# Both attentions of a Trainium2 network: score products issued in pairs, float32 operands kept whole, and the parallel layer's sums of squares by matmul

## The chip, the cores and the metric

The kernel runs on one core of one Trainium2 chip. Its time is the device time of one execution in microseconds (us), and the figure to compare is the median over runs. The engines are named as the profile names them: PE is TensorE, PEld its weight loads, DVE is VectorE, ACT is ScalarE, POOL is GpSimd, SP issues DMAs.

## The reference, cut to what matters

A network of four layers over one sequence of 512 positions with 1,024 features, all in float32, each layer followed by a SwiGLU feed-forward block. Layer 0 is an mLSTM, layer 3 a short convolution; the change does not touch them. Two layers hold an attention.

Layer 1, the window attention (16 query heads of 64, 4 key heads, blocks of 128 queries that see the block before, their own and the next):

```python
scores = jnp.einsum('bcqhgd,bckhd->bchgqk', q, k_band) * (hd ** -0.5)
scores = jnp.where(mask[None, :, None, None], scores, -jnp.inf)
m = jnp.maximum(jnp.max(scores, axis=-1), sink_l)
p = jnp.exp(scores - m[..., None])
denom = jnp.sum(p, axis=-1) + jnp.exp(sink_l - m)
out = jnp.einsum('bchgqk,bckhd->bcqhgd', p, v_band)
```

Layer 2, the parallel layer, runs an attention and a state-space model (SSM) from one input projection. The attention (8 heads of 64, causal) first picks, with 8 small index heads, the 128 best keys of each query, and then attends to those alone:

```python
il = jnp.einsum('bthd,bsd->bths', iq_blk, ik) * (IDX_DIM ** -0.5)
score = jnp.einsum('bths,bth->bts', jax.nn.relu(il), iw_blk)
_, sel = lax.top_k(score, topk)
q_lat = jnp.einsum('bthd,hdc->bthc', q_blk, w_uk)
logits = jnp.einsum('bthc,btkc->bthk', q_lat, c_sel) * (HEAD_DIM_A ** -0.5)
p = jax.nn.softmax(logits, axis=-1)
```

Ahead of layer 2 stand two norms one behind the other: the first block's final norm (weight `fin`) and layer 2's own (weight `par`).

## The kernel before, in words

Activations lie with features on the partitions: `xT[0..7]` are eight tiles of 128 features by 512 positions. A large product is not done in whole float32. Each operand is split into a high and a low part in the rounded type `fp32r` (`whi`/`wlo` for weights, `xh`/`xl` for activations), and three products of these parts stand for one: lines 206 to 208 (`mm3`), 212 to 214 (`mm3n`). Such a product over 512 columns is called a gemm product below, and they are by far the most of PE's work. The splitting costs ACT one pass (line 171) and DVE or POOL another (line 166) for each weight tile.

Products of heads are 64 rows deep. Two heads stand in one tile, one on partitions 0 to 63 and one on 64 to 127 (`halves`).

PSUM's eight banks are dealt to four uses, `g`, `s`, `t` and `o`; `bank(tag)` takes the next bank of a use in turn. `s` holds scores, `t` transposes, `o` attention outputs, `g` gemm products.

**Window attention** (`window`, lines 949 to 1075). `attend(g, c, y)` does four heads for one block `c` of queries: line 1015 multiplies queries by 256 keys (c = 0 and 3) or 384 keys (c = 1 and 2) in whole float32; line 1020 (DVE) adds the mask and takes the row minimum; line 1023 (ACT) is the exponential; line 1027 transposes it block by block; lines 1030 and 1032 copy it out of PSUM (`pT`); line 1036 multiplies by the values, 64 output rows for each of the two halves; lines 1038 to 1050 divide. There are 16 such calls. Six gemm groups (the later queries, `rope`) and six blocks of the output projection (`add_block`) are issued between them and serve PE as other work. In whole float32 one product shows as two PE records.

**Parallel layer** (`parallel`). `norm("par", pre="fin")` makes for each of the eight `xT` tiles two squares on ACT (line 271), two running sums on DVE (line 272), a multiplication by `fin` (line 277) and the split `xh`/`xl` (lines 279, 280). `col_sums` (line 239) adds each running sum over the partitions with four products by a column of ones. From them come two inverse square roots (lines 229 to 234), and `rows` (line 245) spreads these over the partitions as `rb`, which the projection's results are multiplied by. The index weights need a transpose of the first result (line 1124). The index scores (lines 943, 944) use the queries stacked with their low part (lines 929, 930) and the key in two forms (`ikh`, `ikl`). `topk_rounds` picks the best keys on DVE (lines 1176, 1177), a few rounds at a time by `pump`. In the attention itself `att_head(c, h, ...)` does one head for one block: three products of parts for the scores (line 1380), DVE mask and minimum (1381), ACT scale and exponential (1386, 1387), transposes (1391), a split of the result into `pth` (ACT, 1393) and `ptl` (DVE, 1394), and three products of parts by the values for each 128 keys (1402), an odd head with 128 output rows, an even one with 64. `fill` issues gemm groups of the SSM in between.

What is written in one order in the program is not the order on the engines: a scheduler arranges the instructions of all engines by its own estimate of times when the kernel is built. On the chip each engine then goes through its list in that order, and an instruction whose input is not there holds up all behind it.

Of the kernel before, what the change touches and what calls it, by code (L numbers as in the profile page):

```python
# [16 lines left out]
P = 128  # L17
# [40 lines left out]
def tile_net(ctx: ExitStack, tc: tile.TileContext, d, out, layers=(0, 1, 2, 3)):  # L58
# [24 lines left out]

    def bank(tag):
        ids, n = banks[tag]
        banks[tag][1] = (n + 1) % len(ids)
        return pp.tile([P, 512], F32, tag=f"b{ids[n]}", name=f"ps_{tag}", bufs=1)

# [25 lines left out]

    V = nc.vector
# [138 lines left out]

    def norm(wname, pre=None, tag="t", later=False):
# [6 lines left out]
        sums = [scr("ssum", bufs=1)]  # L262
        if pre:
            sums.insert(0, row_tile())
# [9 lines left out]
        for k in range(KT):  # L274
            if pre:
                square(k, sums[0])
                V.tensor_scalar(xT[k], xT[k], col(pre, k), None, op0=ALU.mult)
            hi, lo = xs_pair()
            A.activation(hi, xT[k], AF.Copy, scale=col(wname, k))
            V.scalar_tensor_tensor(lo, xT[k], col(wname, k), hi.bitcast(F32), op0=ALU.mult, op1=ALU.subtract)  # L280
            xs.t.append((hi, lo))
            square(k, sums[-1])
        rcs = []

        def scales():
            for i, ssum in enumerate(sums):
                v = scr("nv", (P, NCH))
                V.tensor_scalar(v, col_sums(ssum, tag), 1.0 / D, None if i else EPS, op0=ALU.mult,
# [658 lines left out]
    def window():  # L947
# [52 lines left out]
        share([1, 3, 3, 1])  # L1000
        halves = slice(0, 64), slice(64, P)

        def attend(g, c, y):
# [8 lines left out]
            for j in range(2):  # L1012
                pss = [bank("s") for _ in halves]
                for a, ps in zip(halves, pss):
                    T.matmul(ps[:, 0:n], lhsT=Q[2 * g + j][a, sl], rhs=K[pair][a, ks], start=True, stop=True)  # L1015
                for r, ps in enumerate(pss):
# [6 lines left out]
                    A.activation(p[:, 0:n], ps[:, 0:n], AF.Exp, scale=-1.0, bias=nmx[:, i:i + 1],  # L1023
                                 accum_out=den[:, i:i + 1])
# [52 lines left out]
    def parallel(after_final):  # L1077
# [3 lines left out]
        QS, CKV, IQ, Z, XBC = 0, 512, 768, 1280, 2304  # L1081

# [37 lines left out]
        V.tensor_tensor(ikw[0:72], p0[0:72], xs.rb[0:72], op=ALU.mult)  # L1120

        cps = bank("t")
        for c in range(NCH):
            T.transpose(cps[:, c * 8:(c + 1) * 8], ikw[64:72, c * P:(c + 1) * P], ident[64:72, 64:72])
        iw = lpool.tile([P, NCH, 8], F32, name="iw")
        V.scalar_tensor_tensor(iw, cps[:, 0:32].rearrange("p (c k) -> p c k", c=NCH), H ** -0.5,
                               xs.rc[:, :, None].to_broadcast([P, NCH, 8]), op0=ALU.mult, op1=ALU.mult)
        ikh, ikl = scr("ikh", dt=F32R, bufs=1), scr("ikl", dt=F32R, bufs=1)
        key_stack(ikw, 0, ikh, ikl)
# [13 lines left out]

        def index(b):
            r = iq[b]
            for par in range(2):
                h = 2 * b + par
                q2 = scr("q2", dt=F32R)
                pair_stack(r, par, q2)
                for c in range(1, NCH):  # L1150
                    n = (c + 1) * P
                    ps = bank("s")
                    scores(ps[:, 0:n], q2, par, ikh, ikl, slice(c * P, (c + 1) * P), slice(0, n))
                    t = scr("rel", bufs=2)
                    A.activation(t[:, 0:n], ps[:, 0:n], AF.Relu, scale=0.125)
# [109 lines left out]
        def keep_q(ps):  # L1265
            hi, lo = keep("N", F32R), keep("N", F32R)
# [476 lines left out]
```

## Time and profile before

| | |
|---|---|
| median of 3 runs | 2445.88 us (2444.16 to 2448.54) |
| profiled execution, its own time | 2444.67 us |
| its span, first to last instruction | 2442.9 us |
| PE busy | 2387.8 us, 98% |
| DVE busy | 1804.2 us, 74% |
| ACT busy | 1198.3 us, 49% |
| POOL busy | 361.2 us, 15% |
| mean granted PE clock | 0.99 of full speed |

The profiled execution is 1.2 us below the median, and 1.8 us of it lie outside the span. A busy PE is not a PE at its peak: a record runs from the start of a product to its modelled end, and records of neighbours overlap. What a product costs PE is therefore read from start to start: the next row's start minus its own.

### The profile page before, as it was taken

How to read it: one execution, taken by the hardware profiler on the slowest of the kernel's cores; microseconds unless marked ns; L12 is line 12 of the kernel's file. 1: busy time of each engine (PE TensorE's matmuls, PEld its weight loads, DVE VectorE, ACT ScalarE, POOL GpSimd, SP SyncE). 2: the span in 40 equal slices, each digit the busy share in tenths (PEclk: the TensorE clock that was granted, in tenths of full speed). 3: DMA queues.
4: the chain of work that ended last, by engine and by line, in shares of the span. 5: the costliest groups of instructions: out<-in, count | busy, mean ns of one | idle time of the engine just before them, and what ended most of it. 6: DMA issues, size and time to landing. Idle time of an engine off the chain costs nothing.

```text
span 2442.9 us, 36706 instructions
## 1 busy us (share of the span) xinstructions
PE 2387.8 (98%) x13956; PEld 2055.9 (84%) x13956; DVE 1804.2 (74%) x3063; ACT 1198.3 (49%) x2226; POOL 361.2 (15%) x252
## 2 busy tenths in 40 slices
PE   8999999999999999999899989999999999999998
PEld 7898899998656899999677867888989788899997
DVE  7676798777564787877789778786867755668877
ACT  4444545454464554545566564553635324445444
POOL 2210001010320001010354145100100010000100
PEclk9999999999999999999999999999999999999999
DMA  5332232323211232323222132232323323223232
GB/s 167 117 100 61 78 117 96 113 87 119 82 51 35 69 113 88 120 87 110 78 71 61 53 111 87 87 100 82 121 87 104 104 96 100 81 88 120 87 104 78
DMA packets 73440, 226.64 MB, mean 93 GB/s; under 512 B 10336, under 2 KB 14576, under 8 KB 73264
## 3 DMA queue, kind: packets, MB, share of 16 engines
q1 hardware_dynamic: 68896, 220.00, 28.0%
q10 hardware_dynamic: 4320, 4.21, 0.6%
q8 instruction: 109, 1.79, 0.3%
q14 instruction: 67, 0.55, 0.1%
q0 software_dynamic: 48, 0.10, 0.0%
HBM read 219.45 MB, written 2.20 MB: 91 GB/s over the span
## 4 chain that ended last, share of the span: by engine, by line
PE 90%; DVE 5%; DMA 2%; ACT 1%; issue 1%; POOL 0%; ACTq 0%; SPq 0%; POOLq 0%; DVEq 0%
PE ps_g L206 7%; PE ps_g L208 7%; PE ps_g L207 7%; PE ps_s L206 4%; PE ps_s L208 4%; PE ps_s L207 4%; PE ps_g L446 4%; PE ps_g L444 4%; PE ps_g L445 4%; PE ps_t L206 3%; PE ps_t L207 3%; PE ps_t L208 3%; PE ps_t L446 3%; PE ps_t L445 3%; PE ps_t L444 3%; PE ps_s L1015 2%
## 5 line engine op out<-in xcount | busy, mean ns | idle before, releaser
L171 ACT ACTIVATE whi<-wraw 128x512 fp32r<-128x512 f32 (+1 forms) x726 | 447.3, 621 | 667.7 <-PE ps_g L207 236.6
L166 DVE TENSOR_TENSOR wlo<-wraw,whi 128x512 fp32r<-128x512 f32 x666 | 490.3, 746 | 188.5 <-ACT whi L171 176.1
L206 PE MATMUL ps_g<-xh,whi 128*128 128x512 f32 (+1 forms) x696 | 279.7, 404 | 2.9 <-DVE ct L1611 2.1
L424 POOL TENSOR_TENSOR S<-wraw 128x1024 f32<-128x1024 f32 x36 | 106.9, 2971 | 1173.3 <-DMA wraw<-in_in_dram 760.3
L207 PE MATMUL ps_g<-xl,whi 128*128 128x512 f32 (+1 forms) x696 | 278.1, 400 | 0.0
L208 PE MATMUL ps_g<-xh,wlo 128*128 128x512 f32 (+1 forms) x696 | 277.8, 399 | 0.0
L171 ACT ACTIVATE whi<-S 128x512 fp32r<-128x512 f32 x288 | 178.2, 628 | 191.3 <-PE ps_g L445 58.2
L166 DVE TENSOR_TENSOR wlo<-S,whi 128x512 fp32r<-128x512 f32 x288 | 199.8, 719 | 34.8 <-ACT whi L171 32.9
L444 PE MATMUL ps_g<-thi,whi 128*128 128x256 f32 x576 | 164.1, 285 | 2.7 <-ACT whi L171 1.9
L446 PE MATMUL ps_g<-thi,wlo 128*128 128x256 f32 x576 | 164.1, 285 | 0.2
L206 PEld LDWEIGHTS ps_g<-xh,whi 128*128 128x128 f32 (+1 forms) x696 | 132.1, 190 | 37.8 <-issue 5.6
L445 PE MATMUL ps_g<-tlo,whi 128*128 128x256 f32 x576 | 163.7, 284 | 0.0
L208 PEld LDWEIGHTS ps_g<-xh,wlo 128*128 128x128 f32 (+1 forms) x696 | 132.0, 190 | 31.6 <-issue 4.4
L207 PEld LDWEIGHTS ps_g<-xl,whi 128*128 128x128 f32 (+1 forms) x696 | 132.2, 190 | 29.1 <-issue 3.5
L444 PEld LDWEIGHTS ps_g<-thi,whi 128*128 128x128 f32 x576 | 111.4, 193 | 3.3 <-ACT whi L171 2.1
L446 PEld LDWEIGHTS ps_g<-thi,wlo 128*128 128x128 f32 x576 | 111.4, 193 | 0.7 <-DVE wlo L166 0.7
L445 PEld LDWEIGHTS ps_g<-tlo,whi 128*128 128x128 f32 x576 | 111.3, 193 | 0.0
L166 POOL TENSOR_TENSOR wlo<-wraw,whi 128x512 fp32r<-128x512 f32 (+1 forms) x60 | 81.0, 1359 | 153.4 <-ACT whi L171 110.5
L207 PE MATMUL ps_s<-hlo,whi 128*128 128x512 f32 x264 | 102.8, 389 | 0.0
L208 PE MATMUL ps_s<-hhi,wlo 128*128 128x512 f32 x264 | 102.7, 389 | 0.0
L206 PE MATMUL ps_t<-hhi,whi 128*128 128x512 f32 x264 | 102.7, 389 | 0.0
L207 PE MATMUL ps_t<-hlo,whi 128*128 128x512 f32 x264 | 102.7, 389 | 0.0
(545 smaller groups left out, 6641.2 us busy)
## 6 DMA issues: line engine op xcount, KB each, us to landing
wraw<-in_in_dram SPq DMA_DIRECT2D x176, 512.0 KB, 3.5
wraw<-in_down_dram SPq DMA_DIRECT2D x82, 512.0 KB, 3.6
wraw<-in_par_in_dram SPq DMA_DIRECT2D x30, 512.0 KB, 3.3
wraw<-in_mlstm_in_dram SPq DMA_DIRECT2D x24, 512.0 KB, 3.6
wraw<-in_sc_in_dram SPq DMA_DIRECT2D x24, 512.0 KB, 3.5
wraw<-in_attn_in_dram SPq DMA_DIRECT2D x12, 512.0 KB, 3.4
wraw<-in_par_out_dram SPq DMA_DIRECT2D x12, 512.0 KB, 3.5
mb<-drs SPq DMA_DIRECT2D x16, 256.0 KB, 4.1
```

The costliest lines, as they stand in the source:

```text
L166: (V if e == "V" else G).tensor_tensor(lo, x, hi.bitcast(F32), op=ALU.subtract)
L171: A.activation(hi, raw, AF.Copy)
L206: T.matmul(o, lhsT=w[0], rhs=x[0], start=start, stop=False)
L207: T.matmul(o, lhsT=w[0], rhs=x[1], start=False, stop=False)
L208: T.matmul(o, lhsT=w[1], rhs=x[0], start=False, stop=stop)
L424: G.tensor_tensor(live[jj, "S1"], live[jj, 2], live[jj, 3], op=ALU.add)
L444: T.matmul(o, lhsT=w[0], rhs=x[i][0], start=start and i == j == 0, stop=False, skip_group_check=True)
L445: T.matmul(o, lhsT=w[0], rhs=x[i][1], start=False, stop=False, skip_group_check=True)
L446: T.matmul(o, lhsT=w[1], rhs=x[i][0], start=False, stop=end, skip_group_check=True)
L1015: T.matmul(ps[:, 0:n], lhsT=Q[2 * g + j][a, sl], rhs=K[pair][a, ks], start=True, stop=True)
```

## The change

It touches both attentions and the entry of the parallel layer.

1. **Pairs.** `side_by_side` issues the score products of two heads (the two halves) one behind the other, at a raised scheduling priority. A dependency is added from each to the instruction that last reads either of their banks (the exponential, or the index heads' ReLU), so that neither starts before both banks are free. `rotate` sets the order in which the `s` banks are taken. In the window attention one bank moves from `t` to `s` (3 and 3 become 4 and 2). In the parallel layer there are three `s` banks, taken as 0 and 1, then 0 and 2.
2. **Whole float32.** In the parallel layer the index scores, attention scores and the products by the values use unsplit operands, each head on its half of the array. The high and low parts of queries, keys, values and probabilities are no longer made. Of two halves the products by the values issue the second first, in both attentions.
3. **Entry.** For `norm("par", pre="fin")` there is one square for each tile instead of two and no running sum. The square itself is the weight side of four small products for each tile, with two columns of weights (ones, and `fin` squared), which add up both sums in PSUM. The split uses one scale, `fin` times `par` (`pcol`, made once at the start on POOL). The multiplication of `xT` by `fin` joins that by the first norm's row and moves into the attention's blocks c = 2 and 3 (DVE, eight instructions, held behind the mask instruction of the pair). The transposes of the index weights move behind the first latent gemm group.

The core of the diff:

```diff
+    def side_by_side(products, tag="s"):
+        tiles, ids = [], []
+        for _ in products:
+            names, n = banks[tag]
+            ids.append(names[n])
+            tiles.append(bank(tag))
+        with tc.high_priority(HP):
+            for f, ps in zip(products, tiles):
+                ins = f(ps)
+                for i in ids:
+                    if i in busy:
+                        tc.add_manual_dep(ins.ins, busy[i].ins.name, SYNC)
+        return list(zip(ids, tiles))
...
-        for k in range(KT):
-            if pre:
-                square(k, sums[0])
-                V.tensor_scalar(xT[k], xT[k], col(pre, k), None, op0=ALU.mult)
...
+        if pre:
+
+            both = bank(tag)
+            for k in range(KT):
+                sq = row_tile()
+                A.activation(sq, xT[k], AF.Square)
+                hi, lo = xs_pair()
+                A.activation(hi, xT[k], AF.Copy, scale=pcol[:, 2 * KT + k:2 * KT + k + 1])
...
+                for c in range(NCH):
+                    T.matmul(both[:, 2 * c:2 * c + 2], lhsT=sq[:, c * P:(c + 1) * P], rhs=pcol[:, 2 * k:2 * k + 2],
+                             start=k == c == 0, stop=k == KT - 1, skip_group_check=True)
...
-        share([1, 3, 3, 1])
+
+        share([1, 4, 2, 1])
+        rotate("s", (0, 1, 2, 3, 1, 0, 3, 2))
...
-                pss = [bank("s") for _ in halves]
-                for a, ps in zip(halves, pss):
-                    T.matmul(ps[:, 0:n], lhsT=Q[2 * g + j][a, sl], rhs=K[pair][a, ks], start=True, stop=True)
-                for r, ps in enumerate(pss):
+                pss = side_by_side([lambda ps, a=a: T.matmul(ps[:, 0:n], lhsT=Q[2 * g + j][a, sl], rhs=K[pair][a, ks],
+                                                             start=True, stop=True) for a in halves])
+                for r, (bid, ps) in enumerate(pss):
...
-                for r, a in enumerate(halves):
+                for r, a in ((1, halves[1]), (0, halves[0])):
...
+        rotate("s", (0, 1, 0, 2))
+
         def index(b):
-            r = iq[b]
-            for par in range(2):
-                h = 2 * b + par
-                q2 = scr("q2", dt=F32R)
-                pair_stack(r, par, q2)
-                for c in range(1, NCH):
-                    n = (c + 1) * P
-                    ps = bank("s")
-                    scores(ps[:, 0:n], q2, par, ikh, ikl, slice(c * P, (c + 1) * P), slice(0, n))
-                    t = scr("rel", bufs=2)
-                    A.activation(t[:, 0:n], ps[:, 0:n], AF.Relu, scale=0.125)
+
+            for c in range(1, NCH):
+                n = (c + 1) * P
+                pss = side_by_side([lambda ps, a=a: T.matmul(ps[:, 0:n], lhsT=iq[b][a, c * P:n], rhs=ik[a, 0:n],
+                                                             start=True, stop=True) for a in halves])
...
-            for i, (x, z) in enumerate(((0, 0), (1, 0), (0, 1))):
-                T.matmul(ps[:, 0:n], lhsT=q[x][a, c * P:n], rhs=k[z][a, 0:n], start=i == 0, stop=i == 2)
...
+            pss = side_by_side([lambda ps, a=a: T.matmul(ps[:, 0:n], lhsT=q[a, c * P:n], rhs=k[a, 0:n],
+                                                         start=True, stop=True) for a in halves])
...
-            A.activation(hi[:, 0:n], pt[:, 0:n], AF.Copy)
-            V.tensor_tensor(lo[:, 0:n], pt[:, 0:n], hi[:, 0:n].bitcast(F32), op=ALU.subtract)
...
+                if par and c >= 2:
+                    V.tensor_copy(t[:, 0:n], pt[:, 0:n])
+                else:
+                    A.activation(t[:, 0:n], pt[:, 0:n], AF.Copy)
...
-                m = P if h % 2 else 64
-                for i, (v, t) in enumerate(((vh, hi), (vh, lo), (vl, hi))):
-                    T.matmul(o[0:m, h // 2 * P:h // 2 * P + P], lhsT=v[:, 0:m], rhs=t[:, sl],
-                             start=j == 0 and i == 0, stop=j == c and i == 2)
+                for par, a in ((1, halves[1]), (0, halves[0])):
+                    T.matmul(o[a, b * P:(b + 1) * P], lhsT=va[j][:, P * b + 64 * par:P * b + 64 * par + 64],
+                             rhs=pts[par][:, sl], start=j == 0, stop=j == c)
...
+                if after_final and c >= 2:
+                    k = 4 * (c - 2) + b
+                    with tc.issue_after(latest[0].ins):
+                        V.scalar_tensor_tensor(xT[k], xT[k], col("fin", k), xs.rb1, op0=ALU.mult, op1=ALU.mult)
```

What the scheduler makes of it, at three places. A row is one instruction as it stands in an engine's list, or so many alike in a row (`x2`); `q_6592` and the like are single tiles of queries and keys.

PE in the gemm-poor middle of the window attention, before (scores line 1015, transposes 1027 and 1047, products by the values 1036):

```order
L1015 MATMUL ps_s<-q_6592,q_6738 128x384
L1027 MATMUL ps_t<-ident,prob 128x128 x6
L1015 MATMUL ps_s<-q_6592,q_6836 128x384 x2
L1047 MATMUL ps_t<-ident,rdb 128x128 x2
L1036 MATMUL ps_o<-pT,va 64x256
L1027 MATMUL ps_t<-ident,prob 128x128 x3
L1015 MATMUL ps_s<-q_6592,q_6738 128x256
L1036 MATMUL ps_o<-pT,va 64x256 x5
```

The same place in the changed kernel, where these lines are 1059 (scores), 1072 and 1092 (transposes) and 1081 (values):

```order
L1059 MATMUL ps_s<-q_6596,q_6840 128x256 x2
L1072 MATMUL ps_t<-ident,prob 128x128 x9
L1059 MATMUL ps_s<-q_6629,q_6958 128x256 x2
L1092 MATMUL ps_t<-ident,rdb 128x128 x2
L1081 MATMUL ps_o<-pT,va 64x256 x6
L1072 MATMUL ps_t<-ident,prob 128x128 x2
```

Over the whole window attention the 64 score products stood alone 41 times, in twos 10 times and once in a three, 52 groups; now twice alone and 31 times in twos, 33 groups. The 80 products by the values stood in groups of 1 (11 times), 3 (6), 4 (2), 5 (5) and 6 (3); now of 1 (once), 3 (once), 4 (7) and 6 (8). The transposes are the same in number.

PE in the parallel attention's last block, before, where two heads of one pair are multiplied by the values (line 1402; 128 output rows for the odd head, 64 for the even one):

```order
L1402 MATMUL ps_o<-ptl,N 128x128
L1402 MATMUL ps_o<-pth,N 128x128 x2
L1402 MATMUL ps_o<-ptl,N 128x128
L1402 MATMUL ps_o<-pth,N 128x128
L1402 MATMUL ps_o<-pth,N 64x128
L1402 MATMUL ps_o<-ptl,N 64x128
L1402 MATMUL ps_o<-pth,N 64x128 x2
L1391 MATMUL ps_t<-ident,prob 128x128 x8
L1380 MATMUL ps_s<-kh,N 128x512 x2
L1380 MATMUL ps_s<-kl,N 128x512
```

In the changed kernel, in the block before the last and at the turn to the last (values 1449, transposes 1439, scores 1424, gemm products 231 to 233):

```order
L1449 MATMUL ps_o<-pth,N 64x128 x6
L1439 MATMUL ps_t<-ident,prob 128x128 x6
...
L1424 MATMUL ps_s<-kh,N 128x512 x2
L231 MATMUL ps_g<-xh,whi 128x512
L232 MATMUL ps_g<-xl,whi 128x512
L233 MATMUL ps_g<-xh,wlo 128x512
L1439 MATMUL ps_t<-ident,prob 128x128 x3
L1449 MATMUL ps_o<-pth,N 64x128 x6
```

Where 240 products by the values stood in runs broken by other work, 80 now stand in groups of 2 (twice), 4 (5 times), 6 (4) and 8 (4), of which each two beside each other are two halves. All 16 score pairs of the attention and all 12 of the index heads stand as twos; the index heads had 24 times two products of parts.

PE at the parallel layer's entry, before, from the first row spread (line 245) to the transposes of the index weights (line 1124):

```order
L245 MATMUL ps_t<-ident,nrc 128x128 x4
L208 MATMUL ps_g<-xh,wlo 128x512
L206 MATMUL ps_g<-xh,whi 128x512
L207 MATMUL ps_g<-xl,whi 128x512
L208 MATMUL ps_g<-xh,wlo 128x512
L245 MATMUL ps_t<-ident,nrc 128x128 x4
L1124 MATMUL ps_t<-ident,ikw 128x8 x4
L206 MATMUL ps_g<-xh,whi 128x512
```

In the changed kernel (small products 317, row spread 270, index scores 1203, gemm products 231 to 233):

```order
L317 MATMUL ps_t<-pcol,rb 128x2 x8
...
L270 MATMUL ps_t<-ident,nrc 128x128 x4
L233 MATMUL ps_g<-xh,wlo 128x512
...
L270 MATMUL ps_t<-ident,nrc 128x128 x4
L231 MATMUL ps_g<-xh,whi 128x512
...
L1203 MATMUL ps_s<-ik,iq 128x256 x2
```

The 32 small products stand in four groups of eight. Behind the last of these come 32 gemm products, the first row spread, 10 gemm products, the second row spread, 33 gemm products and only then the first index scores; the transposes of the index weights stand 15 gemm products later still.

## Rows read from the trace of the kernel before

**Rows 1.** The page: busy time of each engine, share of the span, instructions

```profile
PE 2387.8 (98%) x13956; PEld 2055.9 (84%) x13956; DVE 1804.2 (74%) x3063; ACT 1198.3 (49%) x2226; POOL 361.2 (15%) x252
```

**Rows 2.** Busy time by stretch: window attention, its gemm-poor middle, entry, index and attention

```profile
core 0: us, PE busy (x) PEld busy (x) DVE busy (x) ACT busy (x) POOL busy (x), PEclk, DMA share, GB/s
632.00:796.00 164.00, 158.96 (x739) 95.92 (x739) 91.10 (x248) 91.01 (x266) 33.63 (x22) 0.98 0.17 51
705.60:725.40 19.80, 19.80 (x103) 10.05 (x103) 11.42 (x43) 14.08 (x49) 4.09 (x3) 1.00 0.02 6
1172.00:1212.00 40.00, 32.88 (x149) 26.24 (x148) 32.31 (x62) 17.50 (x31) 15.34 (x11) 0.91 0.26 79
1212.00:1411.00 199.00, 197.55 (x1037) 153.32 (x1037) 161.23 (x380) 124.57 (x283) 73.84 (x61) 0.99 0.20 62
```

**Rows 3.** Timeline of PE in the window attention: start, length, line, records

```profile
713.53 0.70 PE L1015 MATMUL ps_s<-q,q 64*128 64x256 f32 x2
714.16 0.65 PE L1036 MATMUL ps_o<-pT,va 128*64 128x256 f32 x2
714.73 0.44 PE L1027 MATMUL ps_t<-ident,prob 128*128 128x128 f32 x2
...
721.79 1.08 PE L1036 MATMUL ps_o<-pT,va 128*64 128x256 f32 x8
722.80 0.44 PE L1027 MATMUL ps_t<-ident,prob 128*128 128x128 f32 x2
723.17 0.91 PE L1015 MATMUL ps_s<-q,q 64*128 64x384 f32 x2
724.01 0.44 PE L1027 MATMUL ps_t<-ident,prob 128*128 128x128 f32 x2
724.38 0.92 PE L1015 MATMUL ps_s<-q,q 64*128 64x384 f32 x4
725.23 0.44 PE L1027 MATMUL ps_t<-ident,prob 128*128 128x128 f32 x2
```

**Rows 4.** Timeline of PE: one index head, 512 keys, and the gemm product behind it

```profile
1222.09 0.39 PE L943 MATMUL ps_s<-ikh,q 128*128 128x512 f32 x1
...
1222.83 0.50 PE L208 MATMUL ps_g<-xh,wlo 128*128 128x512 f32 x1
```

**Rows 5.** Busy time 1212 to 1411 of lines 1380 (first) and 1402 (second) alone

```profile
1212.00:1411.00 199.00, 19.95 (x96) 11.95 (x96) 0.99 0.20 62
...
1212.00:1411.00 199.00, 26.57 (x240) 24.58 (x240) 0.99 0.20 62
```

**Rows 6.** Timeline of PE: 23 products by the values, then seven halves in the SSM

```profile
1404.04 0.22 PE L1402 MATMUL ps_o<-ptl,N 128*128 128x128 f32 x1
...
1405.94 1.06 PE L1391 MATMUL ps_t<-ident,prob 128*128 128x128 f32 x8
...
1447.14 1.09 PE L1531 MATMUL ps_s<-m,xd 128*64 128x128 f32 x14
1448.16 0.50 PE L207 MATMUL ps_g<-N,whi 128*128 128x512 f32 x1
```

**Rows 7.** Timeline of PE at the parallel entry; brackets: idle before, releaser

```profile
1189.43 0.95 PE L239 MATMUL ps_t<-ones,ssum 128*128 128x1 f32 x8
1190.25 0.48 PE L206 MATMUL ps_g<-xh,whi 128*128 128x512 f32 x1
...
1201.01 0.84 PE L245 MATMUL ps_t<-ident,nrc 128*128 128x128 f32 x4 [4.61 <-DVE nrc L298]
1204.03 0.57 PE L1124 MATMUL ps_t<-ident,ikw 8*128 8x8 f32 x4 [2.18 <-DVE ikw L1120]
```

**Rows 8.** Groups of DVE and ACT by line, 1212 to 1411

```profile
L1394 DVE TENSOR_TENSOR ptl<-ps_t,pth 128x128 fp32r<-128x128 f32 (+3 forms) x32 | 15.1, 483 | 5.3 <-ACT pth L1393 5.2
L1381 DVE CUSTOM_DVE_ANT_0 ps_s<-ps_s,mask 128x128 f32<-128x128 f32 (+3 forms) x32 | 15.4, 494 | 1.2 <-PE ps_s L1380 1.1
L1387 ACT ACTIVATE prob<-ps_s,mx,nrc 128x128 f32<-128x128 f32 (+3 forms) x32 | 19.7, 615 | 0.1
```

More of the change, by code (lines that the diff above doesn't have):

```diff
@@ L82, in share, with rotate @@
             n += m
+    def rotate(tag, order):
+        ids = sorted(set(banks[tag][0]))
+        banks[tag] = [[ids[i] for i in order], 0]
     def bank(tag):
@@ L261, in norm @@
         xs.t = []
-        sums = [scr("ssum", bufs=1)]
-        if pre:
-            sums.insert(0, row_tile())
+        sums = [None, None] if pre else [scr("ssum", bufs=1)]
         def square(k, ssum):
@@ L287, in scales @@
                 v = scr("nv", (P, NCH))
-                V.tensor_scalar(v, col_sums(ssum, tag), 1.0 / D, None if i else EPS, op0=ALU.mult,
+                total = col_sums(ssum, tag) if ssum else both[:, i:2 * NCH:2]
+                V.tensor_scalar(v, total, 1.0 / D, None if i else EPS, op0=ALU.mult,
                                 **({} if i else dict(op1=ALU.add)))
@@ L1081, in parallel @@
         QS, CKV, IQ, Z, XBC = 0, 512, 768, 1280, 2304
+        halves = slice(0, 64), slice(64, P)
         sm = []
@@ L1367, in parallel @@
                 fill()
+        latest = [None]
         ya = []
@@ new lines, in att_pair @@
+            q, k = qk["q"][b], qk["k"][b]
+            pss = side_by_side([lambda ps, a=a: T.matmul(ps[:, 0:n], lhsT=q[a, c * P:n], rhs=k[a, 0:n],
+                                                         start=True, stop=True) for a in halves])
+            pts = []
+            for par, (bid, ps) in enumerate(pss):
+                h = 2 * b + par
+                latest[0] = V.tensor_tensor_reduce(out=ps[:, 0:n], in0=ps[:, 0:n], in1=mask[:, moff[c]:moff[c] + n],
+                                       scale=-0.125, scalar=3.0e38, op0=ALU.add, op1=ALU.min,
+                                       accum_out=mx[:, h:h + 1])
+                p = scr("prob", bufs=PBUF)
+                A.activation(mx[:, h:h + 1], mx[:, h:h + 1], AF.Copy, scale=xs.rc[:, c:c + 1])
+                busy[bid] = A.activation(p[:, 0:n], ps[:, 0:n], AF.Exp, scale=nrc[:, c:c + 1], bias=mx[:, h:h + 1],
+                                         accum_out=den[:, h:h + 1])
+                pt = bank("t")
+                for j in range(c + 1):
+                    T.transpose(pt[:, j * P:(j + 1) * P], p[:, j * P:(j + 1) * P], ident)
+                t = scr("pth", bufs=4)
+                if par and c >= 2:
+                    V.tensor_copy(t[:, 0:n], pt[:, 0:n])
+                else:
+                    A.activation(t[:, 0:n], pt[:, 0:n], AF.Copy)
+                pts.append(t)
```

102 lines of the change are left out of this document (48 added, 54 removed).

## The prediction

> **What bounds the kernel now.** I read the page first: PE is busy for 2387.8 of 2442.9 us, the next engine, DVE, for 74% [rows 1]. So the question is what the change takes from PE's list, and whether another engine then holds PE up. The busy times by stretch say where the change meets what [rows 2]. In the window attention PE works 158.96 of 164 us and DVE and ACT a little over half; nothing but PE binds. In its middle, where few gemm products stand between the attention's small ones, PE never stops, and ACT is at 14.08 of 19.80, 71%: that is the nearest other engine. At the parallel entry PE works 32.88 of 40 us at a mean clock of 0.91. In the index and attention stretch it works 197.55 of 199, with DVE at 161.23, 81%.
>
> PE's prices are read from the timeline, from one row's start to the next. The reader should see in [rows 3] that one score product of 384 keys takes 0.84 us (723.17 to 724.01) and two halves behind each other 0.85 (724.38 to 725.23): the pair is two for one already, where the order has them together. At 256 keys a single takes 0.63, so 128 keys are worth 0.21. Four products by the values, in a row and alternating halves, take 1.01 (721.79 to 722.80), a lone one 0.57. Two equations, in which a "slot" is a lone product or a pair of halves: 2 slots + group = 1.01, 1 slot + group = 0.57, so 0.44 a slot and about 0.14 a group. The seven halves of the SSM check it: 128 columns, four slots at half of 0.44 plus the group make 1.02, and the row says 1.02 [rows 6].
>
> **The change part by part.** Minus is time taken from PE.
>
> *Window scores.* 52 groups become 33. Nineteen groups at the mean of 0.63 and 0.84, that is 0.735, are 14.0; the three-fold one cost a further 0.42 that a pair doesn't: **-14.4**. The work does not change, and the rows price both forms, so I see little doubt in it, 1 us at most.
>
> *Window products by the values.* From the groups counted in the change's section and the order of halves in them: 51 slots in 27 groups become 41 slots in 17. Ten slots and ten groups at 0.44 and 0.14: **-5.8**.
>
> *Index scores.* An index head at 512 keys costs 0.74 for its two products of parts (1222.09 to 1222.83) [rows 4]. A pair at 512 keys is not in the trace; from 0.85 and 0.21 it is 1.06 (bounds: 0.85, if the length counted for nothing, and 1.48, if nothing overlapped). The 12 pairs go over 256, 384 and 512 keys; the same saving of 0.42 holds at each length if both forms scale, so 12 x (2 x 0.74 - 1.06): **-5.0** (0 to -7.6).
>
> *Parallel scores.* Line 1380 is busy 19.95 for 96 records [rows 5]; part of each last record lies beside its follower, for which I take 2 off (an estimate), so 18. Sixteen pairs, four of each length, are 4 x (0.42 + 0.63 + 0.85 + 1.06) = 11.8: **-6.2**.
>
> *Parallel products by the values.* Line 1402's 240 products are busy 26.57 [rows 5]; 23 in a row take 1.90, 0.083 each [rows 6], which gives 19.9 for all. I take 22, between them, since most runs are short. After: 80 halves in 15 groups, 40 slots of 0.215 and 15 x 0.15 are 10.9: **-11.1** (-9 to -15.7).
>
> *Small products.* 32 new ones of two columns stand in place of two sums of four by one column. The old four (eight records) take 0.82 from start to start [rows 7], 0.10 a record; 64 records are 6.6, less the two old groups' 1.64: **+5.0**. From below, the two columns could cost no more than half of it, +1.7; from above, each group may pay a further switch, +6. The old idle row spread shows that DVE had to deliver two running sums first; now PE delivers.
>
> In the Trainium skill's page TensorEngine Tiling (Array Packing), section Instruction Overhead, a product of one column is said to take as long as one of 60. By that, and at the full clock, I estimate 64 records at 1.6 us, and the sum would be 5 us better; the old small products' row is four times dearer than the page has it.
>
> *Entry waits.* The row spread waits 4.61 us for DVE and the transpose of the index weights 2.18 [rows 7]. Both are now issued later: behind the last small products come 42 gemm products, 9.5 us at the 0.225 that they take (0.50 of length, half beside the next), before the second spread. The old chain from the last sum to it, 1190.25 to 1201.01, was 10.8, but DVE did the split of the queries (line 930, removed) inside it; without that I count some 6. So the cover suffices by 3 us, and lacks 1.3 if the chain stays as long. The index weights have 33 gemm products and more. **-6.8.** The clock: 0.91 of 40 us is 3.6 us of PE lost, part of which lies in those waits; I take **-1.5** between 0 and -3.6. DVE's multiplication of eight tiles, 0.7 each, moves from the entry into the attention: nothing on PE's path unless DVE binds.
>
> The squares' buffers are two, so a square waits for the small products two tiles before; between two groups stand 17 gemm products, 3.8 us, against one square on ACT. That cover is ample, and nothing is added. `pcol` is made on POOL, 15% busy: nothing.
>
> The sum: 14.4 + 5.8 + 5.0 + 6.2 + 11.1 - 5.0 + 6.8 + 1.5 = **45.8**.
>
> *What comes back.* First, the window's middle. Its 19.80 us hold 15 score products, so an attend of four heads costs ACT 14.08 / 3.75 = 3.75 us and cost PE 5.28. The two window terms take 20.2 us from 16 calls, 1.26 each, so PE now needs 4.02, and five such calls stand there with hardly a gemm product. ACT is then 93% busy, its queue has a wait in every pair, and `t` has two banks rather than three for the copies behind the transposes. I give back 4 us: five calls at something under one us. Second, the parallel stretch: DVE loses `ptl`'s 15.1 [rows 8] and the splits of index queries and values, and gets eight multiplications and eight copies; if these last weigh about as much as the splits, 146 us remain of the 177 that PE's terms leave of 199, 82% against 81%. What waits there is the pair: bank 0 is in each, so a pair starts only when the pair before has had its minimum (0.494) and exponential (0.615) [rows 8], 1.11 us, and behind it in PE's list stand gemm products that could have run. With gemm products between most pairs I give back 3. So 38.8 net. The profiled execution took 2444.67, 1.2 below the median: 2444.67 - 38.8 = 2405.9, as a median **2407**.
>
> **The rivals.**
>
> *B, another engine holds the pairs.* In the middle ACT binds outright, and half of the parallel waits are open. For it: ACT's 93% there, and the two-bank `t`. Against: outside the middle gemm groups and output blocks stand between the calls, and PE's waits in the window were 5 us in all. Price: the middle goes back to its old pace (5 x 1.26 = 6.3, 2 more than counted) and 28 pairs wait half of 1.11 (16, 13 more than counted): 2422; if the window's other 22 pairs wait as long, 12 more: **2422 to 2434**. The Trainium skill warns of this in the same page, section PSUM Bottleneck: tiling speeds up TensorE, not the reading of PSUM, so that copies may become the bound. The trace as yet shows ACT and DVE below PE in every stretch.
>
> *C, the clock.* Where PE waits, the rows show a clock below 1: 0.91 at the entry, 0.98 in the window [rows 2]; in the middle it is 1.00, with PE never idle. New waits there may bring the lower level, 1.2 GHz, for a stretch. The 20 us of five calls would double at worst, less the waits it absorbs: +13, **2420**. Against it: the other waits cost at most a few us of clock each.
>
> *E, the pairs don't run side by side in the parallel layer.* There each is read from tiles that the trace never shows so used. Each pair would then cost a second single: 11.8 for the 16 and 12 x 0.85 = 10.2 for the 12, and 40 more slots of 0.215 are 8.6: 2407 + 31 = **2438**. Against: the window's own pairs, 0.85 for two, are of the same shape.
>
> *D, slower.* The added dependency binds PE in order. If the waits of all pairs, 31 in the window and 28 in the parallel layer, stay open, 59 x 1.11 = 65, less the 7 counted, is +58: **2465**. It decides from (38.8 + 7) / 59 = 0.78 us a pair on, 70% of the whole chain, in the mean. For it: the instruction waits at the head of PE's list, nothing passes it. Against: only the five calls of the middle lack gemm products between pairs.
>
> **How the numbers follow.** Chances: my forecast, a gain of 26 to 54 us (2392 to 2419), 0.74; B 0.13, C 0.05, E 0.04, D 0.04. The lower end is all bounds that help together: no give-back and the dearer old values, about 2444.67 - 53. The upper end, 2427, takes C and the lower third of B: 0.05 + 0.04, with 0.72 of the 0.74, is about 0.8. A difference under 0.2%, 4.9 us, is about what a measurement of this kernel cannot tell from none; to be within that, D would have to come at two thirds. Faster 0.95, same 0.02, slower 0.03.
>
> **What the changed profile would show.** Line 1059's pairs at 0.63 and 0.85, lines 1203 and 1424 at 1.06 for 512 keys; else E. Line 1449's eight halves at 4 x 0.215 + 0.15 = 1.0. Line 317's eight products at 1.65. No wait ahead of line 270's spreads. In the window's middle ACT above 90% and PE's waits of some 4 us at a granted clock of 1.0; with 0.5 there, C is right. PE's busy total should fall by some 35 to 40 us and its idle time change by little; if busy falls as said and idle grows by as much, B or D is right.

## The result

The changed kernel took 2408.61 us in the median of 4 runs (2404.37 to 2410.95), the kernel before 2445.02: a ratio of 0.9847, 95% interval 0.9835 to 0.9859. Timed a second time, beside other kernels, it took 2404.88 and 2443.14, ratio 0.9843 (0.9830 to 0.9857); one of the five executions of that timing took 11,522 us at a granted clock of 1.0, stands outside the ratio, and nothing here shows what held it up. So it is faster by 1.5%, some 37 us; forecast was 2407. The profiled execution took 2404.37, the shortest of the first four, with a span of 2402.7 us.

The page of the changed kernel, busy time of each engine, to be read against [rows 1]:

```profile
PE 2348.5 (98%) x13892; PEld 2029.1 (84%) x13892; DVE 1758.9 (73%) x2995; ACT 1182.5 (49%) x2194; POOL 355.4 (15%) x251
```

PE lost 39.3 us of busy time and the span 40.2: what it gained is work taken off PE, and its idle time stayed what it was. The windows of the changed kernel, columns as in [rows 2] (window attention, its gemm-poor middle, the feed-forward block behind it, parallel entry, index and attention):

```profile
core 0: us, PE busy (x) PEld busy (x) DVE busy (x) ACT busy (x) POOL busy (x), PEclk, DMA share, GB/s
630.00:776.76 146.76, 138.47 (x748) 89.58 (x748) 85.71 (x249) 90.22 (x266) 34.01 (x23) 0.99 0.18 57
...
695.70:713.60 17.90, 15.98 (x102) 8.37 (x101) 11.79 (x43) 13.29 (x47) 3.05 (x2) 1.00 0.07 26
...
776.76:860.00 83.24, 78.89 (x404) 67.89 (x405) 63.54 (x100) 46.13 (x72) 6.14 (x2) 0.96 0.23 72
...
1157.00:1192.00 35.00, 35.00 (x184) 29.05 (x183) 14.27 (x40) 18.18 (x29) 14.78 (x13) 1.00 0.27 85
1192.00:1380.00 188.00, 181.35 (x941) 130.56 (x939) 148.17 (x351) 113.97 (x263) 69.13 (x56) 0.97 0.21 68
```

The entry now has PE busy throughout at a full clock, where [rows 2] had 32.88 of 40 at 0.91. Two stretches got worse: the feed-forward block, at a granted clock of 0.96 with 4.4 us idle, and the index and attention, with 6.7 idle where there were 1.5. The timeline of the changed kernel says where; the rows also give the prices to hold against [rows 3], [rows 4], [rows 6] and [rows 7]:

```profile
698.25 0.70 PE L1059 MATMUL ps_s<-q,q 64*128 64x256 f32 x4
698.89 0.44 PE L1092 MATMUL ps_t<-ident,rdb 128*128 128x128 f32 x2
...
709.28 0.92 PE L1059 MATMUL ps_s<-q,q 64*128 64x384 f32 x4
710.12 0.44 PE L1092 MATMUL ps_t<-ident,rdb 128*128 128x128 f32 x2
...
839.31 0.39 PE L488 MATMUL ps_t<-thi,whi 128*128 128x256 f32 x1 [2.11 <-ACT whi L196]
...
840.63 0.58 PE L488 MATMUL ps_g<-thi,whi 128*128 128x256 f32 x1 [0.82 <-ACT whi L196]
...
842.85 0.58 PE L490 MATMUL ps_t<-thi,wlo 128*128 128x256 f32 x1 [1.42 <-DVE wlo L191]
...
1151.07 1.98 PEld L317 LDWEIGHTS ps_t<-pcol,rb 128*128 128x128 f32 x16
1151.30 1.84 PE L317 MATMUL ps_t<-pcol,rb 128*128 128x2 f32 x16
1153.00 0.72 PE L233 MATMUL ps_s<-xh,wlo 128*128 128x512 f32 x2
...
1177.49 0.60 PE L270 MATMUL ps_t<-ident,nrc 128*128 128x128 f32 x4
...
1200.13 1.13 PE L1203 MATMUL ps_s<-ik,iq 64*128 64x512 f32 x4
1201.19 0.50 PE L233 MATMUL ps_g<-xh,wlo 128*128 128x512 f32 x1
...
1243.65 1.83 DVE L1212 SCALAR_TENSOR_TENSOR sc<-rel,iw,sc 128x512 f32<-128x512 f32 x1
...
1246.80 0.67 DVE L1325 TENSOR_TENSOR kh<-ps_g,ssum 128x512 f32<-128x512 f32 x1
...
1247.56 0.80 PE L1424 MATMUL ps_s<-kh,N 64*128 64x128 f32 x4 [4.58 <-issue]
...
1360.10 1.09 PE L1449 MATMUL ps_o<-pth,N 128*64 128x128 f32 x16
1361.12 1.09 PE L1439 MATMUL ps_t<-ident,prob 128*128 128x128 f32 x8
```

Pairs cost 0.64, 0.84 and, at 512 keys, 1.06; eight halves 1.02; eight small products 1.70; the row spread has no bracket, so no wait. New are the three waits at 839 to 843 and the one of 4.58 at 1247.56, each settled below.

### The profile page after: what moved, and what is told of

It reads as the page before. It is cut to its first block, busy times and chain, and to the rows that moved or that the text cites. A ratio compares the mean times of both kernels' runs of the same rounds, so it can differ in the third digit from the quotient of the medians.

```text
span 2402.7 us, 36441 instructions
## 1 busy us (share of the span) xinstructions
PE 2348.5 (98%) x13892; PEld 2029.1 (84%) x13892; DVE 1758.9 (73%) x2995; ACT 1182.5 (49%) x2194; POOL 355.4 (15%) x251
## 5 line engine op out<-in xcount | busy, mean ns | idle before, releaser
L233 PE MATMUL ps_t<-hhi,wlo 128*128 128x512 f32 x264 | 102.7, 389 | 0.0
```

The costliest lines, as they stand in the source:

```text
L233: T.matmul(o, lhsT=w[1], rhs=x[0], start=False, stop=stop)
```

## The experiments

Medians are in us; "the changed kernel" is its first median, 2408.6, for the first eight and the second, 2404.9, timed beside them, for the last four. The two timings of this one kernel lie 3.7 apart, and the kernel before lay between 2443.1 and 2445.1 beside all of them, so a smaller difference of medians says little by itself, and the stretch of the trace that the edit touches has to decide. A "place" below is one product that stands alone in PE's list, or two on different halves beside each other: what the prediction calls a slot.

**The window's part alone** (`attend`, the banks and the order of the halves put into the kernel before).

> The kernel before with the window attention's part alone (pairs, four score banks, order of the halves); the parallel layer is as before. Theory (each part is paid for by the PE time that its products need from start to start, and the parts add): the window part is worth 15.6 for scores, 5.6 for values, less 5.3 that the feed-forward block behind it waits in the changed kernel: 2445 - 15 = 2430, between 2424 and 2432. Rival (the window's pairs bring the wait in the feed-forward block only together with the rest, or the parts hinder each other): 2445 - 20 = 2425 without that wait, or less gain than 10 us.

Measured: 2431.38 against 2445.07, ratio 0.9941 (0.9928 to 0.9953), 13.7 us. Its trace has the new waits of the feed-forward block (2.11, 0.82, 1.72), so these come with the window's part, and what remains for the parallel layer is the rest, some 23, by subtraction: that part was not run alone. In the two traces the stretch from the parallel entry to the SSM's end is 26 us shorter in the changed kernel than in this one or the kernel before (430 against 455 and 457).

**Pairs not held together.**

```diff
-        with tc.high_priority(HP):
-            for f, ps in zip(products, tiles):
-                ins = f(ps)
-                for i in ids:
-                    if i in busy:
-                        tc.add_manual_dep(ins.ins, busy[i].ins.name, SYNC)
+        for f, ps in zip(products, tiles):
+            f(ps)
```

> The changed kernel, with the two products of a pair issued without the raised priority and without the added dependency; all else is as changed. In PE's list the window's scores stand in 58 groups (33 with the pairs held together), the index scores need 15 single-or-pair places instead of 12, the attention scores 22 instead of 16. Theory (a place costs the same for one product as for two): 25 x 0.735 + 3 x 0.85 + 6 x 0.74 = 25 us slower than the changed kernel, about 2433. Rival (holding pairs together costs waits that eat the gain, so that most of the gain is from whole float32 and fewer products): within 8 us of the changed kernel.

Measured: 2449.31, 1.0015 (1.0007 to 1.0024) of the kernel before: 40.7 slower than the changed kernel, the whole gain, where 25 was expected. The windows of this kernel, line 1055 (scores) alone, PE busy:

```profile
629.00:801.00 172.00, 48.06 (x128) 17.52 (x128) 0.97 0.16 49
```

The same 64 products are busy 26.79 in the changed kernel's window attention. The scores explain what was expected: from start to start 44.1 against 24.6 in the window, 13.9 against 10.4 for the index and 16.2 against 12.5 for attention, 26.9 in all. The rest I read from the two timelines as 6.4 of idle time and 5.5 of gemm products at the lower clock. Holding the pair is not a detail of the change; without it, the change as a whole gains nothing. The raised priority and the added dependency were taken out together, so which of the two the pair needs is not shown.

**Halves apart in the parallel products by the values.**

```diff
-            for j in range(c + 1):
-                for par, a in ((1, halves[1]), (0, halves[0])):
+            for par, a in ((1, halves[1]), (0, halves[0])):
+                for j in range(c + 1):
```

> The changed kernel, with the parallel layer's products by the values ordered by half (all of the second half, then all of the first) instead of alternating; their number and groups are unchanged. Theory (a half costs nothing only beside the other half): a head pair over n key blocks needs 2n - 1 places of 0.215 us instead of n, 24 more in all: 5.2 us slower, 4 to 9. Rival (the gain in line 1449 is only that 80 products stand where 240 stood): no difference, and groups of eight keep 1.03 us.

Measured: 2411.46 (2407.47 to 2412.0), 2.9 slower, an interval of 0.9843 to 0.9870 that overlaps the changed kernel's. The trace decides. The timeline of a group of eight:

```profile
1364.69 1.58 PE L1449 MATMUL ps_o<-pth,N 128*64 128x128 f32 x16
1366.20 1.09 PE L1439 MATMUL ps_t<-ident,prob 128*128 128x128 f32 x8
```

1.51, against 1.02 alternating. Over all 15 groups 14.1 against 11.0: 3.1, less than the 4 to 9 expected. So the order of the halves matters, and the rival falls; but the count of 2n - 1 places falls too. It makes 0.80, 1.23 and 1.65 for groups of four, six and eight products; from start to start they take 0.59, 1.07 and 1.51, against 0.59, 0.81 and 1.02 alternating. A group of four loses nothing. The starts of the single records show why. Each half runs at 0.109 us a record, and the second half, although all of it stands behind the first in PE's list, starts 0.01 us after it in a group of four, 0.28 in one of six and 0.49 in one of eight: each time when all but three records of the first half have started. From there on the two halves run beside each other. So a product need not stand directly beside its partner; and that PE goes through its list in order holds here within a half, not between the two.

**The old entry** (squares, running sums, `fin` and the row's multiplication as before).

> The changed kernel with the entry of the parallel layer as before: two squares and two running sums for each tile, sums by two groups of four products, multiplication of the tiles by the first norm's weight at the entry and by its row behind the attention. Theory (the small products cost 5.0 of PE and save waits of 6.3 and about 1 of clock): 1 to 4 us slower than the changed kernel, about 2411, with an idle row spread of 3 to 5 us in the trace. Rival (the waits are covered anyway once the index weights stand later and the query splits are gone, so that the small products are a loss): 3 to 6 us faster than the changed kernel, and no wait at the row spread.

Measured: 2410.91 (2410.02 to 2413.82), 0.9861 (0.9846 to 0.9876), 2.3 slower, which the two intervals don't tell apart. The timeline has the waits again:

```profile
1183.78 0.76 PE L270 MATMUL ps_t<-ident,nrc 128*128 128x128 f32 x4 [3.09 <-DVE nrc L331]
...
1186.67 0.80 PE L231 MATMUL ps_g<-xh,whi 128*128 128x512 f32 x1 [2.13 <-DVE ikw L1155]
```

5.2 of wait and a lower clock behind it (0.75 granted from 1186 to 1196, where the changed kernel's entry has 1.00), for 5.2 of small products saved: the theory, at the low end.

**The banks of the last output products.** `share([1, 3, 3, 1])` ahead of the last blocks of the window's output projection, which lie in `s` banks.

> The changed kernel; before the last output products of the window attention the banks are dealt 1, 3, 3, 1 again, as the kernel before has them there, instead of 1, 4, 2, 1. Theory (the feed-forward block's new waits, 4.4 us idle and 2 at the lower clock in the changed trace, come from the four score banks in which the last output products then lie, which changes PE's order at the block's start): PE's list there reads as before again, the waits fall to about 1 us, and the kernel is 4 to 5.5 us faster than the changed one, about 2404. Rival (PE simply reaches the block earlier than DVE and ACT can prepare it, whatever the banks): no difference, and the waits of 2.1, 0.8 and 1.4 us stay.

Measured: 2401.97 (2399.43 to 2406.32), 0.9824 (0.9806 to 0.9842), 6.6 faster than the changed kernel (2.9 faster than its second median). The timeline at the block's start has in place of the three waits:

```profile
844.86 0.39 PE L490 MATMUL ps_t<-thi,wlo 128*128 128x256 f32 x1 [0.51 <-DVE wlo L191]
...
847.60 0.50 PE L231 MATMUL ps_o<-xh,whi 128*128 128x512 f32 x1 [0.45 <-DVE fu L548]
```

From the same gemm product to the same, this stretch takes 29.7 us in the kernel before, 35.1 in the changed one and 29.7 here. The order of PE's first groups in the block is the old one again. So 5.3 us of the window's gain were lost to a bank count that outlived the attention.

**The rounds of key picking later.** They are issued on DVE behind the first key tile (`tc.issue_after`), and the rounds asked for behind two of the query products are no longer asked for there (`pump(4)` becomes `pump(0)`).

> The changed kernel; the rounds that pick the best keys (DVE) are issued only behind the first key tile of the parallel attention, so that four rounds of about 0.9 us that stood ahead of it on DVE come later. Theory (the new wait of 4.6 us ahead of the first attention pair is DVE, late with the key tile behind these rounds): the wait shrinks by 3 us or more; the time by 2 to 4 if the rounds are not missed later, about 2405. Rival (DVE has no room later either: the rounds are then waited for at the second block): the wait moves, no gain or a loss of some us.

Measured: 2413.24 (0.9849 to 0.9882), 4.6 slower. My theory fell: in the timeline the wait is hardly shorter.

```profile
1244.18 2.44 DVE L1212 SCALAR_TENSOR_TENSOR sc<-rel,iw,sc 128x512 f32<-128x512 f32 x2 [1.20 <-ACT rel L1208]
...
1246.71 0.69 DVE L1327 TENSOR_TENSOR kh<-ps_g,ssum 128x512 f32<-128x512 f32 x1
...
1247.51 0.77 PE L1426 MATMUL ps_s<-kh,N 64*128 64x128 f32 x4 [3.99 <-issue]
```

The key tile comes right behind the addition of the last index heads, with no round between. It lies in memory that the index heads' tiles give up. (That this memory is the cause is shown further down, with key tiles that have their own.) And the rounds were missed later: 3.3 us more idle time from the first attention pair to the last product by the values, and 3.5 from there to the SSM's end.

**Small products of two tiles only.** Those of the six tiles between are left out.

> The changed kernel; of the 32 small products at the parallel entry those of six of the eight tiles are left out (so the sums hold two tiles alone), the squares stay. Theory (a record of a small product costs PE 0.10 us and all of it lies on the path): 48 records fewer, 4.8 to 5.2 us faster than the changed kernel, about 2403.5. Rival (a record costs what one of 60 columns at full speed would, 0.025 us, and the rest of the length lies beside other work): 1.2 us faster. Second rival (what PE saves it waits for the row spread): no difference, with a wait at the spread.

Measured: 2401.02 (2394.36 to 2404.63), 0.9815 (0.9794 to 0.9836), 7.6 faster. The timeline of a group of four, and behind it the next:

```profile
1157.14 0.95 PE L317 MATMUL ps_t<-pcol,rb 128*128 128x2 f32 x8
1157.94 0.72 PE L233 MATMUL ps_s<-xh,wlo 128*128 128x512 f32 x2
```

0.80 for eight records, half of 1.70 for sixteen. From the first small product to the first of the index the stretch is 8.6 us shorter, but 14 gemm products, some 3.2 us, have moved out of it; up to the SSM's end it is 5.6 shorter, with 5.2 less in these products. What the medians have beyond that is within their spread. The trace's price holds, and no wait stands at the row spread in its place.

**Small products of 64 columns.**

> The changed kernel; each small product at the entry has 64 columns (the same two weights repeated) instead of two. Theory (the cost of a small product is one per record, whatever its few columns): the groups of eight keep 1.70 us, within 0.2. Rival (it is for a good part columns): 64 columns add as much per record as the trace's transposes of 128 columns suggest, 0.03 us, and a group takes 2.1 or more.

One execution, 2406.63. The timeline:

```profile
1153.21 1.89 PE L317 MATMUL ps_t<-pcol,rb 128*128 128x64 f32 x16
1154.91 0.71 PE L233 MATMUL ps_s<-xh,wlo 128*128 128x512 f32 x2
```

1.70, the same as with two columns: the price is one per record. Whose price it is, this run leaves open. Each record also loads a new 128 x 128 piece of the square as weights, and PEld is busy with these loads for the whole of a group (1.98 us for the sixteen at 1151.07 in the result's timeline, 7.76 for all 64, which take 6.81 from start to start). Few or many columns beside the same weights can't tell the load from the product; no run here has fewer loads for the same products.

**The changed kernel again.**

> The changed kernel itself, timed once more beside the next three, as their yardstick. Expected within 3 us of its first median of 2408.6. If the clock of the window attention differs between executions of one program (1.00 throughout the gemm-poor middle in the first trace, lower for some us in the traces of other kernels that have the same code there), then the times spread over 5 us or more; if that came from the code, the spread would be that of the kernel before, 4 us.

Measured: 2404.88, 3.7 below the first median where 3 was expected, the four executions within the ratio from 2404.47 to 2408.46. With the first four, 2404.4 to 2411.0: 6.6 us of spread, against 2441.3 to 2447.1 for the kernel before in these runs, 5.8. So the spread alone doesn't tell the code from the clock; the traces do (last section).

**Key tiles with memory of their own.**

```diff
-            t = scr("kh", bufs=4)
+            t = scr("kh", bufs=1) if len(qk["k"]) > 2 else mid.tile([P, S], F32, tag="kh", name="kh", bufs=3)
```

> The changed kernel; three of the four key tiles of the parallel attention have memory of their own and no longer lie where the index heads' tiles lay. Theory (the wait of 4.6 us ahead of the first attention pair is the key tile, which DVE can't write before the last index heads, whose memory it takes, are added up): the key tile stands ahead of these on DVE, gemm products come between the last index pair and the first attention pair, the wait falls under 1 us: 3 to 5 us faster than the changed kernel. Rival (the list is bound by DVE there, and the wait comes back at the next pair or product): less than 1 us, with waits of the same sum within 1240 to 1300.

Measured: 2410.62 (2409.03 to 2411.28), 0.9863 (0.9849 to 0.9876), 5.7 slower. The cause was right and the gain was not there: the 4.58 wait is gone, no wait over 0.4 us lies between 1232 and 1300, and the gain comes back as waits in the SSM, of which the timeline shows the largest:

```profile
1425.97 0.79 PE L231 MATMUL ps_g<-N,whi 128*128 128x512 f32 x1 [4.84 <-DVE xT L382]
```

Counted from the first index product, PE's idle time falls by 4.8 us up to the first attention pair and grows by 2.0 in the attention and 3.8 in the SSM. From the first small product to the SSM's end the stretch takes 432.7 us, against 430.1 and 431.6 in the two traces of the changed kernel. So there is no gain: it is the rival, a little further on than I had put it. Why the median is 5.7 higher is not explained; no more than 1.1 to 2.6 of it lies in the stretch that the edit touches.

**Both places.**

> Both mended places together: the banks of the window's last output products as in the kernel before, and the key tiles apart. Theory (two separate waits): the gains add, 8 to 11 us faster than the changed kernel, about 2399. Rival (the key tiles' gain is given back on DVE): the 5 to 6 us of the first alone, about 2403.

Measured: 2401.87 (2398.72 to 2402.56), 0.9825 (0.9812 to 0.9839): 3.0 faster than the changed kernel beside it, which the intervals don't tell apart, and 8.7 faster than with the key tiles apart alone. The gains don't add. In the trace the feed-forward block's waits are gone as with the banks alone, and the stretch from the first small product to the SSM's end takes 432.8 us, 432.7 with the key tiles alone and 432.4 with the banks alone; what is faster is the banks' mend. Alone or with the key tiles it gives 2402, the best median of a kernel here that makes the whole sums.

**Three score banks in the window.** `share([1, 3, 3, 1])` and `rotate("s", (0, 1, 0, 2))`.

> The changed kernel; the window attention keeps 3 score and 3 transpose banks (scores taken as 0, 1, 0, 2), instead of 4 and 2. Theory (the pairs cost the same, the fourth bank only spares the wait for the exponential before): scores and values as in the changed kernel, some more waits in the gemm-poor middle, up to 31 pairs x 0.2 = 6 us, and the feed-forward block's waits gone with the fourth bank, -5: within 3 us of the changed kernel. Rival (with three banks each pair waits for the exponential of the pair before it, 1.1 us for the 12 pairs of the middle): 8 us slower or more.

Measured: 2403.79, 0.9836 (0.9822 to 0.9849), 1.1 faster than the changed kernel: no difference that counts. PE's waits in its window attention:

```profile
PE ps_s L1059 <- ACT prob L1068: 5.4, 7, 2.1
```

and those of the changed kernel, of which the first lies at the attention's start, in the kernel before too:

```profile
PE ps_t L1072 <- ACT prob L1068: 3.4, 1, 3.4
PE ps_t L1072 <- ACT pT L1077: 1.6, 6, 0.3
```

With three banks the pairs do wait for the exponential, 5.4 us; with four the transposes wait for the copies, 1.6. PE is busy 82.30 of the 84 us from 776 on, where the changed kernel had 78.89 of 83.24 in that block. What the fourth bank saves, the feed-forward block lost, so that both come to the same.

## Why the prediction was right

The sum was made of PE's prices from start to start. Counted the same way in the changed trace (each group's start to the next row's start, idle time apart), in us:

| term | forecast | measured | |
|---|---|---|---|
| window scores | -14.4 | -15.6 | 40.2 to 24.6 |
| window values | -5.8 | -5.6 | 26.0 to 20.3 |
| index scores | -5.0 | -5.1 | 15.5 to 10.4 |
| parallel scores | -6.2 | -5.6 | 18.1 to 12.5 |
| parallel values | -11.1 | -10.5 | 21.6 to 11.0 |
| small products | +5.0 | +5.0 | 9.8 to 14.8, all sums |
| entry waits | -6.8 | -6.3 | 7.2 to 0.9 |
| rest of the window | +4 | +1.4 | |
| feed-forward block behind it | 0 | +5.3 | 29.7 to 35.1 |
| clock and rest, entry to SSM | +1.5 | -5.0 | |
| all else | 0 | +1.8 | |
| sum | -38.8 | -40.2 | |

The first seven, by which the forecast stands, are each within 1.2 us in this trace; the second trace of the changed kernel has 25.3 for the window's scores and 21.4 for its values, which leaves both terms within 1.3. That a place costs the same for one as for two is what the pairs not held together show from the other side: with 25 more places in the window, 44.1 us of scores.

Both give-backs were sized too large. I had ACT at 93% of the middle. It is 13.29 of 17.90 us there, 74%, and PE's waits in this stretch are 1.9 us, for the copies out of PSUM and not for a pair. The Trainium skill's page TensorEngine Tiling (Array Packing), section PSUM Bottleneck, from which rival B had its backing, warns of those copies, for a speed-up of four times; at the two halves of this case the trace agrees in the kind and bounds the size. The five calls without gemm products that I counted were rather three and a half, seven pairs: gemm products come again from 713.6 on. The prediction's own count of 15 score products there made 3.75. In the parallel layer the pairs' waits that I gave 3 us for came as one wait of 4.6 (5.7 idle in all from the first index product to the first attention pair), and PE's idle time in the attention and the SSM shrank by 4.8 (1.4 to 0.5 and 17.4 to 13.5). That one wait is for the key tile and its memory, not for a pair's banks.

What the prediction did not have is the feed-forward block's 5.3. I read the bank change as one of the attention alone; it held on to the attention's last output products, and that moved the order of PE's groups in a block that no line of the change touches. That the forecast still met the median is partly luck: this loss and the missing give-backs cancel.

The small products were the term at which rule and row parted. By the Trainium skill's page TensorEngine Tiling (Array Packing), section Instruction Overhead, a product of one column lasts as long as one of 60. The 64 columns at an unchanged 1.70 agree. Its figure is not the price here: 0.106 us a record, against the 0.025 that I estimate from it at the full clock, and the products left out gave back the trace's price. Each record here comes with a weight load of its own, and no run tells whether the load or the product sets that price.

Rival C was right in part: from 690 to 710 the granted clock is 1.00 in the first trace and 0.91 in the second of the same kernel (last section). E and D did not come: every pair stands at the price of one, and the pairs' waits, with three banks even, are 5.4 us for 31.

## What to carry to other kernels

Price a PE instruction from start to start, in the place where it stands, and count the places that a change leaves; let products on the two halves alternate (two of one half ahead of two of the other cost nothing here, three or four did); waits that are added to keep two half-array products together can be paid for many times over by the places they save. After a change of banks or pools, look at the next stage too: its order is decided by what is still occupied. And where several engines are nearly full, a wait that is mended at one place is not won before the stage behind has been read.

## What the runs showed of the hardware

The same list of PE instructions was granted different clocks in different executions. The windows of the changed kernel, columns as in the result's windows:

```profile
632.00:650.00 18.00, 14.54 (x59) 9.96 (x59) 12.67 (x25) 10.15 (x28) 7.78 (x5) 0.91 0.38 118
...
690.00:710.00 20.00, 18.30 (x113) 10.21 (x111) 13.25 (x44) 14.88 (x50) 6.01 (x5) 1.00 0.13 40
```

of the same kernel timed again, which reaches its first score product 1.8 us later:

```profile
632.00:650.00 18.00, 14.45 (x50) 9.63 (x51) 11.77 (x23) 10.38 (x27) 6.76 (x5) 0.81 0.43 125
690.00:710.00 20.00, 18.23 (x98) 11.07 (x98) 11.96 (x36) 12.63 (x40) 7.83 (x5) 0.91 0.13 41
```

and of the kernel with the halves apart, which has the same code up to there and reaches it 1 us earlier:

```profile
632.00:650.00 18.00, 14.57 (x53) 9.55 (x52) 12.93 (x24) 9.03 (x24) 8.15 (x6) 0.81 0.37 113
...
690.00:710.00 20.00, 18.00 (x104) 10.08 (x102) 11.72 (x38) 13.16 (x42) 5.91 (x4) 0.91 0.14 40
```

Full speed is 2.4 GHz and the lower level 1.2, so a granted clock of 0.91 or 0.81 is a stretch with some time at each. From its first score product to its last the window attention takes 133.3 us in the first trace, 136.2 in the second of the same kernel and 136.4 in that of the halves apart. PE's idle time in it is alike, 6.3, 6.4 and 6.6 us; what differs is the rest, 127.0, 129.7 and 129.8. In the traces of six more kernels with the same PE list there it ran from 133.5 to 136.2. The two levels can cost or spare about 3 us in one stage from one execution to the next, as much as several of the edits here are worth, so that such edits are better judged by the stretch that they touch than by two medians. Why the clock fell further in the one than in the other, the traces don't show.

Products on the two halves of the array don't start strictly in list order. With all of one half ahead of the other in PE's list, the second half's first record started 0.49 us after the first half's in a group of eight products, while three of the first half's eight records had yet to start; in a group of four products (four records a half) it started 0.01 us after, and the group took the 0.59 us of alternating halves.
